# A hybrid decoder layer on one core: start-up transfers, two projection tiles ahead of the norm, and the within-chunk products of RWKV and HGRN spread over four array quarters

## The chip, the cores and the metric

One core of one Trainium2 chip runs the whole program. The metric is device time in microseconds (us); the median of the runs counts. The engines are named as the profile names them: PE is TensorE's matmul stream, PEld its weight loads, DVE VectorE, ACT ScalarE, POOL GpSimd, SP the queue that issues the DMAs. Each engine runs its own instructions in a fixed order.

## The reference

One decoder layer over a prompt of 2048 tokens and 8 single-token samples, width 1024, all in float32:

```python
h = rmsnorm(x, norm_mix)
p = h @ w_in                                   # 1024 -> 31 tiles of 128 columns, and 12 columns more (b and a of GDN)
y_a = gdn_mixer(p_a); y_b = rwkv_mixer(p_b); y_c = hgrn_mixer(p_c)
x = x + concat(y_a, y_b, y_c) @ w_out
h = rmsnorm(x, norm_ffn)
x = x + (silu(h @ w_gate) * (h @ w_up)) @ w_down
y = rmsnorm(x, norm_final)
```

The three mixers are recurrences with heads of 64, done in chunks of 64 tokens (6, 6 and 4 heads). GDN and RWKV need per chunk the inverse of a unit triangular 64x64 matrix, and all three need products of one chunk's tokens with the same chunk's tokens under a causal mask (in the reference of HGRN: `att = einsum('bhid,bhjd,bhijd->bhij', q, k, dec)`, then `att @ v`). GDN starts with a causal convolution over four tokens, and RWKV mixes each token with the one before, so both look back over the border of a group of tokens; ahead of the first token there are zeros.

## The kernel before

**Tiling.** Tokens stand on the free axis, in four groups q of 512 (the last has the 8 samples as well: 520, as two column ranges of 260). The input projection has 31 tiles m of 128 output columns for each q. A gemm tile (gemm8, L377 to L379) is 8 slices k of the contraction by 3 matmuls, since each float32 operand is split into a high and a low part (hi by hi, hi by lo, lo by hi; 128x512 each); ACT makes the high part of a weight (L332) or of x (L409), DVE the low one (L333, L410). Its result p is multiplied by the norm's 1/rms on DVE (L473) and stored to DRAM (s_p, L480), from where the units load slices. The statistics of the norm (stats_x) are eight squares added up (L456, L460), split (L495, L496) and summed over partitions by matmuls with ones (pni, L499 and L500), then Ln and Exp on ACT (L297, L300). In the same function stand the twelve extra columns (psb, L438, four column strips of the array; then the chain `ba`).

**Units.** For each q there are 3 GDN units (names in _g), 3 RWKV units (_r) and 2 HGRN units (_h); a unit has two heads, one on partitions 0 to 63, one on 64 to 127. Its chunk products are 64x64 or 64x128 matmuls in plain float32, each of which stands as two records in the trace. The matmul of head h reads rows of its half, and its result lies in the half of the output partitions that the head after it needs: a quarter of the array (row half, column half). RWKV: `att` (L1035) is run twice in a row, once for a3 (bank pa, same halves, so the two quarters of one diagonal), then, after the inverse is started, for k3 (bank pk, halves swapped: the other diagonal); each runs twice over four chunks and is masked by DVE (L1052, L1054). HGRN: 5 levels, each with 8 chunks of two 64x64 products (pl, L260 by `pair`), all on one diagonal, into one bank that DVE copies under a mask (L1217).

**Order.** A Driver interleaves the units with the gemm stream. In a turn each live unit goes one step (to its next yield), and then the gemm stream makes products until it has RATES[q] more (12.25 to 19.25 matmuls per turn). A scheduler fixes the order on each engine from that. When all units have ended, the rest of the gemm stream (late) runs by itself, with weights in the units' T buffers; until then gemms come from three banks (tag g) and S buffers.

**Start.** dram() sets 3 columns of zeros before each projected tile of q = 0 by one DMA (L205, 12 bytes at a time, `s_p<-zero`). Then SP issues what the program's text and the scheduler order: the first weight, x, constants, the sample buffers (cbuf, pbuf, o_cs), weights of w_out, x of q = 1, and only then tile 1's weights.

## Time and profile before

| | us |
|---|---|
| median of 3 runs (3198.95 to 3200.74) | 3200.33 |
| profiled execution, its own time | 3198.47 |
| span of that execution | 3196.7 |
| PE busy | 3085.4 (97%) |
| DVE busy | 2192.8 (69%) |
| ACT busy | 1189.0 (37%) |
| mean granted clock of TensorE | 0.983 |

The time lies 1.8 us above the span; the median lies 1.9 us above the profiled execution. A matmul's duration in the rows holds its way through the array, so successive ones overlap: what one costs is the distance of their starts. In rows of a timeline, x16 is the number of records that stand together, and the time in brackets is the idle time before them and who ended it.

### The profile page before, as it was taken

The page shows a single profiled execution, that of the slowest core. Times are in us where ns is not written, and L with a number is a line of the kernel's source. Part 1 is how long each engine was busy: PE and PEld are TensorE (multiplying, and loading weights), DVE is VectorE, ACT ScalarE, POOL GpSimd, SP SyncE. Part 2 cuts the span into 40 slices and gives each one's busy share as a digit, 9 for nine tenths or more (in the row PEclk, how much of TensorE's full clock was granted, in tenths as well). Part 3 has the DMA queues.
Part 4 walks back from the last instruction along what each step waited for, and adds up shares of the span by engine and source line. Part 5 has one row for each costly group of instructions (what it writes and reads, how often), then busy time and mean ns, then how long its engine had stood idle before and what let it go on. Part 6 is the DMA issues. An engine that isn't in the chain of part 4 may idle for free.

```text
span 3196.7 us, 62530 instructions
## 1 busy us (share of the span) xinstructions
PE 3085.4 (97%) x24812; PEld 2469.9 (77%) x24812; DVE 2192.8 (69%) x5369; ACT 1189.0 (37%) x2056; POOL 10.2 (0%) x21
## 2 busy tenths in 40 slices
PE   5989999999999999999999999999999999999998
PEld 3767767777888767677777777777777778999998
DVE  4885666678667788986898887778766654443334
ACT  3543143235325444644365435254532312221002
POOL 0000000000000000000000000000000000000000
PEclk8989999999999999999999999999999999999999
DMA  9958657656655766677775445565645456755552
GB/s 233 333 187 272 186 177 215 187 167 183 198 162 184 229 212 204 221 226 251 227 226 185 162 158 170 168 184 183 205 162 165 149 207 210 249 173 185 185 185 90
DMA packets 393074, 628.06 MB, mean 196 GB/s; under 512 B 176653, under 2 KB 181005, under 8 KB 392781
## 3 DMA queue, kind: packets, MB, share of 16 engines
q1 hardware_dynamic: 391692, 622.99, 61.0%
q8 instruction: 195, 3.19, 0.4%
q10 hardware_dynamic: 1088, 1.07, 0.1%
q14 instruction: 99, 0.80, 0.1%
HBM read 456.79 MB, written 167.19 MB: 195 GB/s over the span
## 4 chain that ended last, share of the span: by engine, by line
PE 79%; DVE 9%; DMA 6%; ACT 3%; SPq 1%; issue 1%; DVEq 0%; ACTq 0%
PE psp L377 7%; PE psp L378 7%; PE psp L379 7%; PE pd L377 5%; PE pd L378 5%; PE pd L379 5%; PE pfu L378 5%; PE pfg L377 4%; PE pfu L377 4%; PE pfu L379 4%; PE pfg L378 4%; PE pfg L379 4%; PE pso L378 1%; PE pso L377 1%; PE pso L379 1%
## 5 line engine op out<-in xcount | busy, mean ns | idle before, releaser
L377 PE MATMUL psp<-xs,w_in 128*128 128x512 f32 (+1 forms) x1240 | 446.3, 360 | 29.2 <-ACT xs L409 17.5
L378 PE MATMUL psp<-xs,w_in 128*128 128x512 f32 (+1 forms) x1240 | 445.9, 360 | 0.3 <-DVE xs L410 0.3
L379 PE MATMUL psp<-xs,w_in 128*128 128x512 f32 (+1 forms) x1240 | 442.9, 357 | 0.8 <-DVE w_in L333 0.8
L377 PEld LDWEIGHTS psp<-xs,w_in 128*128 128x128 f32 x1240 | 235.5, 190 | 72.6 <-ACT xs L409 19.7
L379 PEld LDWEIGHTS psp<-xs,w_in 128*128 128x128 f32 x1240 | 235.6, 190 | 39.5 <-issue 4.4
L378 PEld LDWEIGHTS psp<-xs,w_in 128*128 128x128 f32 x1240 | 235.4, 190 | 39.1 <-issue 2.9
L591 DVE TENSOR_TENSOR x<-pd,x 128x512 f32<-128x512 f32 (+1 forms) x240 | 138.3, 583 | 115.6 <-PE pd L379 113.9
L377 PE MATMUL pfg<-xhs,w_wg 128*128 128x512 f32 x496 | 201.8, 407 | 3.9 <-ACT w_wg L332 2.3
L379 PE MATMUL pfu<-xhs,w_wu 128*128 128x512 f32 x496 | 198.7, 401 | 1.4 <-DVE w_wu L333 1.2
L378 PE MATMUL pfg<-xhs,w_wg 128*128 128x512 f32 x496 | 198.6, 400 | 0.7 <-DVE xhs L549 0.7
L378 PE MATMUL pfu<-xhs,w_wu 128*128 128x512 f32 x496 | 199.2, 402 | 0.0
L377 PE MATMUL pfu<-xhs,w_wu 128*128 128x512 f32 x496 | 198.6, 400 | 0.3 <-ACT w_wu L332 0.3
L379 PE MATMUL pfg<-xhs,w_wg 128*128 128x512 f32 x496 | 198.0, 399 | 0.8 <-DVE w_wg L333 0.8
L377 PE MATMUL pd<-u,w_wd 128*128 128x512 f32 x464 | 188.3, 414 | 6.4 <-ACT u L362 2.3
L378 PE MATMUL pd<-u,w_wd 128*128 128x512 f32 x464 | 187.2, 404 | 0.4 <-DVE u L363 0.2
L379 PE MATMUL pd<-u,w_wd 128*128 128x512 f32 x464 | 185.1, 400 | 0.0
L570 ACT ACTIVATE t<-t 128x512 f32<-128x512 f32 (+1 forms) x110 | 60.0, 546 | 305.3 <-DVE t L569 301.7
L286 ACT ACT_TABLE_LOAD x91 | 116.8, 1283 | 113.6 <-PE oss_g L276 22.1
L362 ACT ACTIVATE u<-t 128x512 fp32r<-128x512 f32 (+1 forms) x110 | 59.9, 545 | 221.1 <-DVE t L573 220.2
L473 DVE TENSOR_TENSOR p<-psp,ri 128x512 f32<-128x512 f32 (+1 forms) x155 | 90.3, 583 | 73.2 <-PE psp L379 71.3
L572 DVE SCALAR_TENSOR_TENSOR t<-pfu,rf 128x512 f32<-128x512 f32 (+1 forms) x110 | 64.2, 583 | 102.9 <-PE pfu L379 100.0
L569 DVE TENSOR_TENSOR t<-pfg,rf 128x512 f32<-128x512 f32 (+1 forms) x110 | 64.2, 584 | 91.3 <-PE pfg L379 83.2
(638 smaller groups left out, 7368.9 us busy)
## 6 DMA issues: line engine op xcount, KB each, us to landing
w_in<-sw_in SPq DMA_DIRECT2D x186, 512.0 KB, 3.9
w_wg<-sw_wg SPq DMA_DIRECT2D x80, 512.0 KB, 3.5
w_wu<-sw_wu SPq DMA_DIRECT2D x80, 512.0 KB, 3.3
w_wd<-sw_wd SPq DMA_DIRECT2D x72, 512.0 KB, 3.3
sw_in<-w_in SPq DMA_DIRECT2D x62, 512.0 KB, 5.1
s_p<-p SPq DMA_DIRECT2D x93, 256.0 KB, 4.3
sw_wg<-w_wg SPq DMA_DIRECT2D x44, 512.0 KB, 2.9
sw_wu<-w_wu SPq DMA_DIRECT2D x44, 512.0 KB, 3.7
```

The source lines that it names most:

```text
L286: p = self.nc.scalar.preload_act_table_set("natural_log_exp_and_others")
L362: nc.scalar.activation(out[:, 0], src, AF.Copy)
L377: nc.tensor.matmul(ps, lhsT=hi[:, ws], rhs=xs[:, 0, xc], start=start, stop=False)
L378: nc.tensor.matmul(ps, lhsT=hi[:, ws], rhs=xs[:, 1, xc], start=False, stop=False)
L379: nc.tensor.matmul(ps, lhsT=lo[:, ws], rhs=xs[:, 0, xc], start=False, stop=stop)
L473: nc.vector.tensor_tensor(p[:, c0:c0 + cn], ps, rstd[q][:, c0:c0 + cn], ALU.mult)
L569: nc.vector.tensor_tensor(g, psg, r[:, cs], ALU.mult)
L570: nc.scalar.activation(t, g, AF.Tanh, scale=0.5)
L572: nc.vector.scalar_tensor_tensor(p, psu, 0.5, r[:, cs], ALU.mult, ALU.mult)
L591: nc.vector.tensor_tensor(x2[d][:, c0:c0 + cn], ps, x2[d][:, c0:c0 + cn], ALU.add)
```

## The change

1. **No zeros through DRAM.** The DMA in dram() goes; slice_p sets the 1 or 3 columns ahead of the group by a memset on POOL where q is 0, and loads only the 512 columns.
2. **Order of the first transfers.** The load of x of the next group moves to just ahead of the second unit's tiles (i == 1); it, the sample buffers and each first load of weights other than w_in's are issued only behind `mark`, the last s_p store made so far.
3. **Two tiles ahead.** For q = 0 the matmuls of the first two projection tiles stand ahead of stats_x in the program's text; their results are held in two banks until 1/rms is there. The buffers of pba, be and ba for q = 0 come from T instead of S.
4. **Four quarters.** RWKV's two products over four chunks are issued together, a diagonal into bank pa and the other into pk, by turns; HGRN's even chunks go on one diagonal into pl0, the odd ones on the other into pl1. Each RWKV unit has two yields fewer. HGRN's masked copy is split into two (even and odd chunks), and so are the copies into W.

```diff
-        zero = self.T("zero")[:, 0:HALO * N_IN]
-        self.nc.vector.memset(zero, 0.0)
-        self.nc.sync.dma_start(self.s_p[0][:, :, 0:HALO].rearrange("m p j -> p m j"),
-                               zero.rearrange("p (m j) -> p m j", j=HALO))
...
-                nc.sync.dma_start(raw, src[:, 512 * i:512 * i + 512])
+                with ExitStack() if key[0] == "in" else self.tc.issue_after(self.mark.ins):
+                    nc.sync.dma_start(raw, src[:, 512 * i:512 * i + 512])
...
-        p = self.S(f"pba{q}")
+        new = self.S if q else self.T
+        p = new(f"pba{q}")
...
-                ps = self.gemm8(w, xs[q], c0, cn, f"psp{q}_{m}_{c0}")
+                ps = held[0] if held else self.gemm8(w, xs[q], c0, cn, f"psp{q}_{m}_{c0}")
...
-            nc.sync.dma_start(self.s_p[q][m, :, HALO:], p[:, :n])
+            self.mark = nc.sync.dma_start(self.s_p[q][m, :, HALO:], p[:, :n])
...
-        self.nc.sync.dma_start(p[:, 0:halo + G], self.s_p[q][m, :, HALO - halo:HALO + G])
+        none = halo if q == 0 else 0
+        if none:
+            self.nc.gpsimd.memset(p[:, 0:none], 0.0)
+        self.nc.sync.dma_start(p[:, none:halo + G], self.s_p[q][m, :, HALO - halo + none:HALO + G])
...
+            for c0 in range(0, GC, 4):
+                cs = slice(c0, c0 + 4)
+                pa, pk = (self.ps(f"p{x}_{nm}").rearrange("p (c w i) -> p c w i", w=2, i=C) for x in "ak")
+                for c in range(4):
+                    for ps, l3, swap in ((pa, a3, 0), (pk, k3, 1)):
                         for h in range(2):
-                            p, o = slice(64 * h, 64 * h + 64), 64 * (h ^ swap)
-                            nc.tensor.matmul(ps[o:o + 64, c], lhsT=l3[p, c0 + c], rhs=rk[p, :, c0 + c],
+                            nc.tensor.matmul(ps[H[h ^ swap], c], lhsT=l3[H[h], c0 + c], rhs=rk[H[h], :, c0 + c],
                                              start=True, stop=True)
...
-                ps = ch(self.ps(f"pl_{nm}"))
+                ps = [self.ps(f"pl{i}_{nm}")[:, :G // 2].rearrange("p (c i) -> p c i", i=C) for i in range(2)]
                 for c in range(GC):
-                    self.pair(lambda p: ps[p, c], lambda p: x3[p, c], lambda p: x3[p, c])
-                nc.vector.copy_predicated(att, self.bc(self.msk[:, n]), ps)
+                    for h in range(2):
+                        nc.tensor.matmul(ps[c % 2][H[h ^ c % 2], c // 2], lhsT=x3[H[h], c], rhs=x3[H[h], c],
+                                         start=True, stop=True)
+                for i in range(2):
+                    nc.vector.copy_predicated(att[:, i::2], self.bc(self.msk[:, n], GC // 2), ps[i])
...
-            if q < 3:
-                load[q + 1] = K.load_x(q + 1)
+            held = []
             for i, (ms, _) in enumerate(order):
+                if i == 1 and q < 3:
+                    with K.tc.issue_after(K.mark.ins):
+                        load[q + 1] = K.load_x(q + 1)
...
+                        held = [K.gemm8(w, xs[q], 0, G, f"psp{q}_{m}")]
+                        w2 = K.load_w(K.io["w1"][ms[1]], ("in", ms[1]), 0)
+                        second = K.gemm8(w2, xs[q], 0, G, f"psp{q}_{ms[1]}")
                         K.load_consts()
+                        K.proj((q,), m, xs, rstd, None, lambda: K.stats_x(0, load[0]), held)
+                        held, w = [second], None
```

**SP at the start.** Before, the rows from tile 0's x to tile 1's first weight (rw_in_0_384; raw_x_262 to 271 are x of q = 1; sw_in is the split weight that is stored for later groups):

```order
L331 DMA rw_o_0_12234<-wo 128x512
L331 DMA rw_o_0_12241<-wo 128x512
L188 DMA blk<-blk 128x256
L194 DMA msk<-msk 128x320
L397 DMA raw_x_262<-xT 128x512 x2
L397 DMA raw_x_265<-xT 128x512 x2
L397 DMA raw_x_268<-xT 128x512 x2
L397 DMA raw_x_271<-xT 128x512 x2
L476 DMA s_p_148<-p_0_274 128x3
L480 DMA s_p_147<-p_0_274 128x512
L756 DMA s_be_142<-be_351 6x512
L331 DMA rw_in_0_384<-w 128x512
```

Here tile 1's weights stand behind the stores of p and be (L476 to L756). After, from the second half of x on:

```order
L337 DMA sw_in_0_1_221<-w_in_0_216 128x1024
L394 DMA raw_x_232<-xT 128x512 x2
L328 DMA rw_in_0_285<-w 128x512
L328 DMA rw_in_0_292<-w 128x512
L186 DMA cst<-cst 128x352
L188 DMA blk<-blk 128x256
L190 DMA w2a_113<-w 64x384
L191 DMA w2a_113<-a 64x384
L192 DMA g_114<-g 128x384
L194 DMA msk<-msk 128x320
L420 DMA wba<-wba 128x8x12
L328 DMA rw_in_0_412<-w 128x512
```

Tile 1's weights (rw_in_0_285, 292) follow x directly, the constants and wba follow them, and the loads of x for q = 1, of the sample buffers and of w_out have left this stretch.

**PE at the start.** Before, from the end of tile 0 (psp_0) to the start of tile 1:

```order
L377 MATMUL psp_0_0_275<-xs_7_259,w_in_0_219 128x512
L438 MATMUL psb_0_337<-raw_x_226,wba 12x512 x2
L438 MATMUL psb_0_337<-raw_x_229,wba 12x512 x2
L438 MATMUL psb_0_337<-raw_x_232,wba 12x512 x2
L438 MATMUL psb_0_337<-raw_x_235,wba 12x512 x2
L378 MATMUL psp_0_0_275<-xs_7_259,w_in_0_219 128x512
L379 MATMUL psp_0_0_275<-xs_7_259,w_in_0_219 128x512
L499 MATMUL pni_330<-sqhi_326,ones 128x512
L500 MATMUL pni_330<-sqli_327,ones 128x512
L377 MATMUL psp_1_0_398<-xs_0_238,w_in_0_383 128x512
```

After, the same place:

```order
L375 MATMUL psp_0_259<-xs_7_256,w_in_0_216 128x512
L376 MATMUL psp_0_259<-xs_7_256,w_in_0_216 128x512
L374 MATMUL psp_1_298<-xs_0_235,w_in_0_284 128x512
L375 MATMUL psp_1_298<-xs_0_235,w_in_0_284 128x512
L436 MATMUL psb_0_371<-raw_x_223,wba 12x512 x2
L436 MATMUL psb_0_371<-raw_x_226,wba 12x512 x2
L436 MATMUL psb_0_371<-raw_x_229,wba 12x512 x2
L436 MATMUL psb_0_371<-raw_x_232,wba 12x512 x2
L376 MATMUL psp_1_298<-xs_0_235,w_in_0_284 128x512
L374 MATMUL psp_1_298<-xs_1_238,w_in_0_284 128x512
```

The statistics' matmuls (pni) stood ahead of tile 1; now 22 matmuls of tile 1 stand ahead of them, and psb stands in tile 1.

**PE in an RWKV unit.** After, two groups of four chunks of one unit (pa_r_2805 is the first, pa_r_2886 the second; before, pa and pk of a group stood apart everywhere); first the end of the interleaved one and the start of the other:

```order
L1052 MATMUL pk_r_2806<-kr_r_2606,kr_2603 64x128 x2
L1052 MATMUL pa_r_2805<-kr_r_2606,a_r_2554 64x128 x2
L1052 MATMUL pk_r_2806<-kr_r_2606,kr_2603 64x128 x2
L1052 MATMUL pa_r_2805<-kr_r_2606,a_r_2554 64x128 x2
L1052 MATMUL pk_r_2806<-kr_r_2606,kr_2603 64x128 x2
L374 MATMUL psp_5_0_4450<-xs_2_3299,w_in_1_4445 128x512
L256 MATMUL pS_r_2872<-SA_r_1980,bt_r_1473 64x64 x2
L375 MATMUL psp_5_0_4450<-xs_2_3299,w_in_1_4445 128x512
L714 MATMUL pj_g_2742<-N_g_1993,uT_g_2515 32x32 x16
L1052 MATMUL pa_r_2886<-kr_r_2606,a_r_2554 64x128 x8
L376 MATMUL psp_5_0_4450<-xs_2_3299,w_in_1_4445 128x512
```

Its second diagonal comes some twenty rows further on:

```order
L1128 MATMUL po_r_3406<-W_r_1303,Z_r_1278 64x64
L1105 MATMUL px_r_2910<-Z_r_1278,W_r_1301 64x64
L1052 MATMUL pk_r_2887<-kr_r_2606,kr_2603 64x128 x8
L1105 MATMUL px_r_2910<-Z_r_1279,W_r_1302 64x64
L1128 MATMUL po_r_3406<-W_r_1304,Z_r_1279 64x64
```

So one group goes by turns over four quarters, and the other as two runs of one diagonal each.

**PE at the end of the units.** Before, the last HGRN level of the last unit (pl_h) and an RWKV chunk step (px_r):

```order
L379 MATMUL pd_7_28274<-u_12_27880,w_wd_3_2_28258 128x512
L377 MATMUL pd_7_28274<-u_13_27984,w_wd_3_2_28258 128x512
L378 MATMUL pd_7_28274<-u_13_27984,w_wd_3_2_28258 128x512
L379 MATMUL pd_7_28274<-u_13_27984,w_wd_3_2_28258 128x512
L260 MATMUL pl_h_28295<-lv_h_28250 64x64 x3
L1101 MATMUL px_r_28288<-Z_r_26158,W_r_26383 64x64
L1101 MATMUL px_r_28288<-Z_r_26159,W_r_26384 64x64
L260 MATMUL pl_h_28295<-lv_h_28250 64x64 x13
L377 MATMUL pfg_14_28322<-xhs_0_25377,w_wg_2_28313 128x512
```

After, the last steps of the same units up to the first gemm behind them (pfg_12, the gate product of the first tile that takes its weights hw_wg from T buffers):

```order
L1223 MATMUL pl_h_27890<-lv_h_27859 64x64 x8
L1223 MATMUL pl_h_27891<-lv_h_27859 64x64 x8
L1128 MATMUL po_r_28054<-W_r_25776,Z_r_25720 64x64
L1105 MATMUL px_r_27817<-Z_r_25720,W_r_25774 64x64
L1105 MATMUL px_r_27817<-Z_r_25721,W_r_25775 64x64
L1128 MATMUL po_r_28054<-W_r_25777,Z_r_25721 64x64
L725 MATMUL ptk_h_27999<-cst,kx_h_27958 128x128 x4
L256 MATMUL pv_r_27830<-X_r_27820,N_r_25772 64x64 x2
L256 MATMUL pS_r_27854<-SA_r_26827,bt_r_26151 64x64 x2
L1128 MATMUL po_r_28054<-W_r_25776,Z_r_25720 64x64
L1105 MATMUL px_r_27883<-Z_r_25720,W_r_25774 64x64
L1105 MATMUL px_r_27883<-Z_r_25721,W_r_25775 64x64
L1128 MATMUL po_r_28054<-W_r_25777,Z_r_25721 64x64
L374 MATMUL pfg_12_28427<-xhs_0_26006,hw_wg_2_28378 128x512
```

Before, gemms (pd_7, pfg_14) stand on both sides of the units' rows; after, 75 rows of units with no gemm among them end here, and the units end at tile 11 of the feed-forward of q = 2 instead of tile 17.

## Rows read from the trace of the kernel before

**Rows 1.** The page: busy time of the engines, and three lines of the 40 slices of the span (tenths of each slice; PEclk is the granted clock).

```profile
PE 3085.4 (97%) x24812; PEld 2469.9 (77%) x24812; DVE 2192.8 (69%) x5369; ACT 1189.0 (37%) x2056; POOL 10.2 (0%) x21
...
PE   5989999999999999999999999999999999999998
...
DVE  4885666678667788986898887778766654443334
...
PEclk8989999999999999999999999999999999999999
```

**Rows 2.** The page: the chain that ended last, shares by engine.

```profile
PE 79%; DVE 9%; DMA 6%; ACT 3%; SPq 1%; issue 1%; DVEq 0%; ACTq 0%
```

**Rows 3.** Timeline of SP's issues, 0 to 50 us (start, duration, line, operation, output from input, count). Here and in the other timelines rows of one kind in a row are one line.

```profile
3.25 0.38 SPq L205 DMA_DIRECT2D s_p<-zero  x1
3.68 8.69 SPq L397 DMA_DIRECT2D raw_x<-xT  x2
...
32.32 4.30 SPq L397 DMA_DIRECT2D raw_x<-xT  x8
44.27 0.33 SPq L476 DMA_DIRECT2D s_p<-p  x1
...
45.59 2.30 SPq L331 DMA_DIRECT2D rw_in<-w  x4
```

**Rows 4.** Timeline of PE, 2 to 62 us.

```profile
7.27 0.79 PE L377 MATMUL psp<-xs,w_in 128*128 128x512 f32 x1 [7.27 <-ACT xs L409]
...
21.51 0.80 PE L377 MATMUL psp<-xs,w_in 128*128 128x512 f32 x1 [7.90 <-ACT xs L409]
...
28.40 1.91 PE L438 MATMUL psb<-raw_x,wba 128*12 128x512 f32 x16
...
38.02 0.80 PE L499 MATMUL pni<-sqhi,ones 128*128 128x512 f32 x1 [7.05 <-DVE sqhi L495]
...
49.98 0.79 PE L377 MATMUL psp<-xs,w_in 128*128 128x512 f32 x1 [9.85 <-ACT w_in L332]
...
59.23 0.40 PE L378 MATMUL psp<-xs,w_in 128*128 128x512 f32 x1
```

**Rows 5.** Timeline of DVE, 5 to 62 us.

```profile
28.98 3.88 DVE L460 TENSOR_TENSOR acci<-acci,sqi 128x512 f32<-128x512 f32 x5 [0.29 <-ACT sqi L456]
...
37.56 0.41 DVE L495 CAST sqhi<-acci 128x512 fp32r<-128x512 f32 x1
...
43.55 0.69 DVE L473 TENSOR_TENSOR p<-psp,ri 128x512 f32<-128x512 f32 x1
```

**Rows 6.** Windows of 10 us from 0 to 80 us: length, busy time of each engine with count, granted clock, DMA share, GB/s; the sum is that of all eight.

```profile
30.00:40.00 10.00, 2.42 (x8) 0.87 (x4) 7.94 (x14) 2.69 (x5) 0.00 (x0) 0.80 0.93 272
40.00:50.00 10.00, 0.15 (x2) 0.02 (x1) 3.88 (x7) 7.66 (x10) 0.00 (x0) 0.50 0.46 143
...
sum 80.00, PE 43.96 PEld 29.56 DVE 38.39 ACT 28.42 POOL 1.01; mean PE 5.50 PEld 3.69 DVE 4.80 ACT 3.55 POOL 0.13
```

**Rows 7.** Windows of the stretch 166 to 197 us, the same columns.

```profile
166.00:176.00 10.00, 9.02 (x235) 6.07 (x235) 9.65 (x21) 4.86 (x9) 0.00 (x0) 1.00 0.14 37
176.00:186.00 10.00, 4.89 (x80) 3.38 (x73) 9.76 (x28) 4.17 (x8) 0.00 (x0) 0.67 0.16 18
186.00:197.00 11.00, 7.22 (x60) 5.02 (x59) 10.72 (x30) 7.89 (x13) 0.00 (x0) 0.50 0.52 157
```

**Rows 8.** Timeline of PE in that stretch: its first row, a run of one diagonal, and the first gemm behind it.

```profile
165.96 0.60 PE L724 MATMUL ptv_r<-cst,vr 128*128 128x128 f32 x4
...
172.58 1.09 PE L1045 MATMUL pk_r<-kr_r,kr 64*64 64x128 f32 x16
...
196.96 0.79 PE L377 MATMUL psp<-xs,w_in 128*128 128x512 f32 x1
```

**Rows 9.** Timeline of PE, 594 to 597 us: an HGRN level, and a GDN product on the other diagonal (it is the product pv, whose halves are swapped).

```profile
595.00 0.27 PE L260 MATMUL pl_h<-lv_h 64*64 64x64 f32 x1
595.00 0.27 PE L888 MATMUL pv_g<-X_g,N_g 64*64 64x64 f32 x2
...
595.12 1.60 PE L260 MATMUL pl_h<-lv_h 64*64 64x64 f32 x47
```

**Rows 10.** Timeline of PE, 700 to 712 us: two gemm matmuls, a small product, and the next gemm matmul.

```profile
708.81 0.40 PE L378 MATMUL psp<-xs,w_in 128*128 128x512 f32 x1
709.04 0.39 PE L379 MATMUL psp<-xs,w_in 128*128 128x512 f32 x1
709.37 0.33 PE L260 MATMUL pv_r<-X_r,N_r 64*64 64x64 f32 x4
709.63 0.50 PE L377 MATMUL psp<-xs,w_in 128*128 128x512 f32 x1
```

**Rows 11.** The instructions of the tile pa_r (engine, operation, count, duration in ns least/median/most, first and last start, shapes); pk_r has as many.

```profile
L1045 PE MATMUL pa_r<-kr_r,a_r x384: 269/269/320, 169.4 to 2394.1; 64*64 64x128 f32 x192
```

**Rows 12.** The instructions of the tile pl_h, and of the copy from it.

```profile
L260 PE MATMUL pl_h<-lv_h x1280: 218/218/364, 595.0 to 2604.5; 64*64 64x64 f32 x183
L1217 DVE COPY_PREDICATED att_h<-msk,pl_h x40: 685/727/759, 596.3 to 2604.8; 128x512 f32<-128x512 uint8 x40
```

**Rows 13.** Windows of 80 us in the mix of units and gemms, and near its end.

```profile
1280.00:1360.00 80.00, 74.95 (x628) 55.49 (x626) 72.12 (x167) 48.91 (x81) 0.00 (x0) 1.00 0.71 226
...
2560.00:2640.00 80.00, 80.00 (x587) 62.19 (x586) 44.82 (x105) 11.28 (x19) 0.31 (x1) 1.00 0.59 206
```

More of the change, by code (lines that the diff above doesn't have):

```diff
@@ L752, in ba @@
         h = slice(0, 12)
-        a, b = p[h, :n], self.S(f"be{q}")[h, :n]
+        new = self.S if q else self.T
+        a, b = p[h, :n], new(f"be{q}")[h, :n]
         nc.scalar.activation(b, a, AF.Tanh, scale=0.5)
@@ L757, in ba @@
         nc.vector.tensor_scalar(a, a, self.par("dtb")[h], None, ALU.add)
-        w1, w2, w3 = (self.S(f"ba{q}_{i}")[h, :n] for i in range(3))
+        w1, w2, w3 = (new(f"ba{q}_{i}")[h, :n] for i in range(3))
         made = nc.vector.scalar_tensor_tensor(w1, a, -1.0, a, ALU.mult, ALU.min)
@@ L1036, in first @@
             fb = f[:, :, None].to_broadcast([128, GC, C])
-            def att(l3, swap, outs, name):
-                for c0 in range(0, GC, 4):
-                    ps = self.ps(f"p{name}_{nm}").rearrange("p (c w i) -> p c w i", w=2, i=C)
-                    for c in range(4):
+            N, Rb = (ch(self.T(f"{n}_{nm}")) for n in ("N", "Rb"))
+            W = [[ch(self.T(f"W{w}{h}_{nm}")) for h in range(2)] for w in range(2)]
+            for c0 in range(0, GC, 4):
[3 more added lines that the diff above has]
+                    for ps, l3, swap in ((pa, a3, 0), (pk, k3, 1)):
@@ L1055, in att, with out @@
-                    yield
-            NR = [ch(self.T(f"{n}_{nm}")) for n in ("N", "Rb")]
-            yield from att(a3, 0, lambda w: ((NR[w], slice(0, 128)),), "a")
-            N, Rb = NR
+                def out(to, ps, w, p):
+                    m = lambda x: x[p, None, :].to_broadcast([p.stop - p.start, 4, C])
+                    if w == 0:
+                        nc.vector.tensor_tensor(to[:, cs], ps[p, :, w], m(self.nstrict), ALU.mult)
+                    else:
+                        nc.vector.scalar_tensor_tensor(to[:, cs], m(self.neg), 0.0, ps[p, :, w], ALU.is_ge, ALU.mult)
@@ L1060, in first @@
+                for w, to in enumerate((N, Rb)):
+                    out(to, pa, w, slice(0, 128))
+                for w in range(2):
+                    for h in range(2):
+                        out(half(W[w], h, True), pk, w, H[1 - h])
+                yield
             inv = self.inverse(N, ("r", u, q), nm)
@@ L1062, in first @@
             yield
-            W = [[ch(self.T(f"W{w}{h}_{nm}")) for h in range(2)] for w in range(2)]
-            yield from att(k3, 1, lambda w: [(half(W[w], h, True), slice(64 - 64 * h, 128 - 64 * h))
-                                             for h in range(2)], "k")
             nc.vector.tensor_tensor(k3, k3, fb, ALU.mult)
@@ L1224, in first @@
                 nc.vector.tensor_tensor(half(W, h), ch(q)[H[h]], ch(eb)[H[h]], ALU.mult)
-                nc.vector.tensor_copy(half(W, h, True), att[H[h]])
+                for i in range(2):
+                    nc.vector.tensor_copy(half(W, h, True)[:, i::2], att[H[h ^ i], i::2])
             ends = self.sp.tile([128, GC], F32, tag="he", name=f"he_{nm}")
@@ L1514, in gemm @@
                 for m in ms:
-                    K.proj((q,), m, xs, rstd, w, lambda: K.stats_x(0, load[0]))
                     if w:
+                        held = [K.gemm8(w, xs[q], 0, G, f"psp{q}_{m}")]
+                        w2 = K.load_w(K.io["w1"][ms[1]], ("in", ms[1]), 0)
+                        second = K.gemm8(w2, xs[q], 0, G, f"psp{q}_{ms[1]}")
                         K.load_consts()
-                    w = None
+                        K.proj((q,), m, xs, rstd, None, lambda: K.stats_x(0, load[0]), held)
+                        held, w = [second], None
+                    else:
+                        K.proj((q,), m, xs, rstd, None, None, held)
+                        held = []
                     have[0] += 1
```

20 lines of the change are left out of this document (7 added, 13 removed).

## The prediction

> **What bounds the kernel now.** I read the page first: PE is busy 3085.4 of 3196.7 us, so 111 us are idle and the rest goes only if PE's own work gets shorter [rows 1]. The chain that ended last says the same, 79% of it on PE and 9% on DVE [rows 2]. The slices show where the idle time is: PE starts at 5 tenths, and DVE is at 8 or 9 tenths in the middle [rows 1]. The windows of the first 80 us have PE busy for 43.96, so 36 of the 111 us are lost there [rows 6]. A second hole is at 166 to 197 us, 31 us without a gemm, in which PE's windows add up to 21.1 of 31 us while DVE is busy 30.1 of 31 [rows 7, 8]. The other 65 us or so are spread over the mix, where DVE comes near its limit: PE 74.95 of 80 us with DVE at 72.12, but 80 of 80 with DVE at 44.82 [rows 13]. So three prices matter: the start, PE's work in small products, and stretches in which DVE paces.
>
> **The start.** The timeline of SP shows x held up: the two issues behind the zeros' DMA take 8.69 us [rows 3]. PE waits for x until 21.51, then for the squares until 38.02, and then for tile 1's weights until 49.98 [rows 4]; these are issued at 45.59, behind x of q = 1 (4.30 us) and the store of p at 44.27 [rows 3]. Without the zeros, 3 MB (two weight tiles and x) at the 272 GB/s of the window from 30 us [rows 6] need 11 us from 2 us on: x is in at about 12 and split at 14. The squares then need what they need now, from the last of x's matmuls near 27 to 37.56, about 10.4 us [rows 4, 5], and some 2.5 us more, since ACT and DVE split tile 1's weights in between: 27. From the first of the statistics' matmuls to p of tile 0 it is now 38.02 to 43.55, 5.5 us [rows 4, 5], so p comes at about 32.5. By then tile 1's 24 matmuls (11 us even at twice the warm spacing of 0.23 [rows 10]) are done beside the squares, and tile 2 can use tile 0's bank at 33. Before, tile 2 is where PE stands at 59.2 [rows 4]. That is 26 us; 4 off for a cold clock (0.80 and 0.50 in the windows in which PE waits [rows 6]) and for the split of the next weights: **-22**, from -12 (if psb, whose weights now come behind the constants, and the squares hold tile 1 up) to -30 (if the statistics don't stretch). The memsets on POOL, idle all but 10.2 us [rows 1], cost nothing. Nor do the transfers that move behind the last store: x of q = 1 is first read by the statistics that end in the hole at 166 us, the sample buffers later still; on SP they now stand behind more weights. The T buffers of the ba chain take it off the S buffers into which SP loads raw weights.
>
> **The hole at 166 us.** After's order has 48 steps of units without a gemm there instead of 33, but 195 matmuls for 188. At 30.1 us of DVE for 79 instructions [rows 7], 0.38 each, some dozen more on the chain are **+5** (0 to +10).
>
> **Four quarters.** A full-array product of 128 columns costs about 0.11 us a record (4 in 0.60, less the last one's way of 0.27), and a 64x128 record on a diagonal 55 ns (16 in 1.09, less 0.27, over 15) [rows 8]: two quarters run at once already. An HGRN record costs 30 ns (47 in 1.60, less 0.22, over 46) [rows 9]. That four run at once the trace shows at one place only: at 595.00 records of pl_h and of pv_g, on the other diagonal, start in the same hundredth [rows 9]. If they do, a record's price halves: RWKV has 2 x 384 records [rows 11], 768 x 27 ns = 21 us, HGRN 1280 x 15 ns = 19 us [rows 12]. But only what stands by turns in the order gains. Counted through PE's order, about 7 of 24 RWKV groups' worth does (the others are two runs of eight, as in the example), 6.3 us, and 27 of 40 HGRN levels, 12.6 us: **-19**, from 0 (not at once) to -25.
>
> The Trainium skill, "TensorEngine Tiling (Array Packing)", Restrictions and Gotchas, says that different row tiles cannot access the same PSUM bank at the same time. The pairs of pk_r write one bank from two row halves and go at half the full array's price [rows 8], so it doesn't hold in this trace for a diagonal. By the rule each of the two banks would take one quarter at a time, the sum would lose the 19, and the time would be that of rival E.
>
> **Fewer interruptions.** A pair between two gemm matmuls takes 0.59 us from start to start instead of 0.23, 0.36 more; its four records at 30 ns are 0.12 of that, so each change of shape costs about 0.12 [rows 10]. PE's order has 1457 such changes after for 1552 before: 95 x 0.12 = **-11** (-5, if DVE paces at those places, to -20, if the pairs' own latency goes too).
>
> **DVE in a shorter mix.** The masked copies become 80 of half the width for 40 of 727 ns [rows 12], and 16 copies become 32: between nothing and 29 us more DVE work, and I take 8, for a half costs more than half. With 24 turns fewer some 380 gemm matmuls (24 x 16, near 89 us) leave the mix for the late stretch, so the same DVE work stands in less time. PE idles 5 us in 80 where DVE is at 72, and none at 45 [rows 13]; four per cent more load on the some 900 us between give **+8** (0 to +20). That both banks of a lane are now filled in one step, so the next step's products wait for the masks, is in this term.
>
> **The uncovered end of the units.** Before, gemms stand on both sides of the last levels, and PE is busy 80 of 80 us at 2560 to 2640 [rows 13]. After, the 75 rows up to pfg_12 have no gemm: pfg_12's weights need T buffers that the units free last, and their loads stand on SP behind the stores of y_g and of the HGRN state. Their DVE chain is some 60 to 90 instructions. At the 0.38 us of the hole [rows 7] that is 23 to 34 us; PE's own work in it is 9 us: **+15**, from +8 (part of it hidden by records of the units themselves) to +25.
>
> **Sum.** -22 + 5 - 19 - 11 + 8 + 15 = -24 against the profiled 3198.5, or 3174.5; the median lies 1.9 above it, so **3176**.
>
> **Rivals.** A is the forecast, with its terms some 15 us either way: 3160 to 3192.
>
> B, the uncovered stretches cost little: DVE +0, hole +0, end +8, the rest as in the sum: -44, 3156; with the start and the interruptions at their best (-30, -20) 3139. For it speaks that DVE is at 69% in the mean [rows 1]; against it that the hole of 166 us is DVE-paced now [rows 7].
>
> C, DVE decides: what PE saves in products is not on the path where DVE is at 72 of 80 [rows 13], and DVE +20, hole +10, end +25 stand against the 52 of gains: 3203. For it speaks that the added copies are on DVE. The Trainium skill, same page, Performance Considerations, says that tiling speeds TensorE and not the emptying of PSUM, which may become the bottleneck; the rows show this only where DVE is above some 65 of 80.
>
> D, slower by the gemm-less end alone: fewer turns let the units outlive their gemms. With the other terms as forecast (-39) it must cost over 45 us to pass 3206.7, that is, a stretch of 54 us with 9 us of PE in it. At the hole's pace, 31 us for 33 steps [rows 7, 8], its 45 steps are 42 us, 33 lost: 3194. It needs a third more than that pace, as when the weights' loads wait and the clock falls to the 0.50 of 186 to 197 us [rows 7]: 3210.
>
> E, the change doesn't do what it says: four quarters don't run at once; the quarters' term is 0: 3195.
>
> **How the numbers follow.** A 0.58, B 0.14, C 0.12, D 0.08, E 0.08. A difference under 0.2% (6.4 us) can hardly be told from none here. Faster (below 3193.9) are A, B, and a third of E and C: 0.79. Within are most of the rest of E and half of C: 0.11. Slower are D and a little of C: 0.10. The range 3146 to 3198 leaves out D, most of C and B's best end, together about 0.2.
>
> **What would show it.** Start: PE busy in the first 80 us rises from 44 to about 64, tile 2's matmuls begin near 33, and no wait for w_in precedes tile 1. Quarters: a run of pa and pk by turns takes some 27 ns a record, 16 ns for pl; if 55 and 30, E. End: a gap in the gemms around 2500 us, about 24 us long, with DVE full; if over 50, D. DVE: windows at 1280 to 1360 with PE below 73 would speak for C. The forecast is wrong if the start's wait moves to the squares or psb as a whole, or if the new order opens holes in the mix that the old one had not.

## The result and the profile after

The changed kernel takes 3220.23 us in the median of four runs (3218.68 to 3222.8), the kernel before 3199.64 on the same chip; the ratio is 1.007, with a 95% interval of 1.0053 to 1.0088. Measured a second time it was 1.0063 (1.0048 to 1.0078). So the change is slower by 21 us where 24 us faster was forecast. Measured again beside each group of experiments, the kernel before had medians of 3190 to 3194 us; each ratio is to the one beside it. Executions of one kernel differ by up to some 20 us, the shorter ones with the higher mean granted clock (e13 below: 3166 and 3168 us at 0.986, the other five 3176 to 3182 us at 0.981 or 0.982), and each split below is that of one profiled execution.

The page after, with the lines that answer to [rows 1, 2]:

```profile
PE 3079.2 (96%) x24812; PEld 2464.1 (77%) x24812; DVE 2194.7 (68%) x5424; ACT 1176.6 (37%) x2051; POOL 12.1 (0%) x41
...
PE   8999999989998999999999999999999899999998
...
PEclk9989999999998999999999999999999899999999
...
PE 68%; DVE 14%; DMA 9%; ACT 4%; issue 2%; SPq 2%; DVEq 0%; ACTq 0%
```

PE is busy 6 us less, and its share of the chain is 11 points less, while DVE's, DMA's and issue's shares have grown. A busy PE is not PE at full speed, so I split each trace into windows of 5 us and counted as lost in each: the idle time of PE, and its busy time times (1 - granted clock), called cold below. What is left is work at full clock. By stage, in us:

| profiled execution | span | 0-80 | 80-240 | 240-2480 (mix) | 2480-2880 (end of the units) | from 2880 | work at full clock |
|---|---|---|---|---|---|---|---|
| before | 3196.7 | 39.5 | 18.2 | 69.8 | 6.7 | 12.7 | 3049.7 |
| after | 3218.8 | 14.6 | 23.0 | 107.2 | 43.6 | 12.2 | 3018.2 |
| difference | +22.1 | -24.9 | +4.8 | +37.4 | +36.9 | -0.5 | -31.5 |

Three of the forecast's terms are there: the start (-22 forecast, -24.9), the hole at 166 us (+5, +4.8) and PE's work (-19 and -11 forecast, -31.5). Two stages eat it all, the mix and the end. Of the mix's +37.4, 13.0 us lie at 1000 to 1070 us (18.4 lost after, 5.4 before), in the hole that is read below; the other 24 are spread, 10 of them at 640 to 800 us (19.2 against 9.4). In idle time and cold clock, the mix lost 49.1 + 20.7 before and 75.5 + 31.8 after.

**The start.** Windows, and PE's and DVE's timelines of the changed kernel, against [rows 4 to 6]:

```profile
10.00:20.00 10.00, 7.60 (x22) 5.02 (x21) 5.76 (x10) 6.71 (x13) 0.00 (x0) 1.00 1.01 318
20.00:30.00 10.00, 8.94 (x39) 4.96 (x40) 9.86 (x18) 3.31 (x6) 0.00 (x0) 0.83 0.96 350
30.00:40.00 10.00, 10.00 (x45) 8.10 (x44) 5.88 (x11) 7.00 (x10) 0.00 (x0) 1.00 0.87 333
```

```profile
8.36 0.79 PE L374 MATMUL psp<-xs,w_in 128*128 128x512 f32 x1 [8.36 <-ACT xs L406]
...
21.06 0.80 PE L374 MATMUL psp<-xs,w_in 128*128 128x512 f32 x1 [3.16 <-ACT w_in L329]
...
22.22 2.96 PE L436 MATMUL psb<-raw_x,wba 128*12 128x512 f32 x16
...
30.33 0.39 PE L500 MATMUL pni<-sqhi,ones 128*128 128x512 f32 x1
...
30.79 0.39 PE L374 MATMUL psp<-xs,w_in 128*128 128x512 f32 x1
```

```profile
25.59 0.42 DVE L496 CAST sqhi<-acci 128x512 fp32r<-128x512 f32 x1
...
34.57 1.29 DVE L471 TENSOR_TENSOR p<-psp,ri 128x512 f32<-128x512 f32 x2
```

Tile 1 starts at 21.06 instead of 49.98, tile 2 at 30.79 directly behind the statistics' matmuls (it doesn't wait for p of tile 0, as the forecast had it), and that p comes at 34.57 instead of 43.55 (32.5 was forecast). All 24 matmuls of tile 1 stand ahead of the statistics'. Tile 1 still waits 3.16 us for its weights, where the forecast had no such wait as a sign of being right. PE is busy 66.8 us of the first 80, for 44 before.

**The quarters.** An HGRN level of the changed kernel on PE, and its masked copy:

```profile
578.37 0.69 PE L1223 MATMUL pl_h<-lv_h 64*64 64x64 f32 x32
```

```profile
L1226 DVE COPY_PREDICATED att_h<-msk,pl_h x80: 412/442/455, 580.0 to 2566.2; 128x256 f32<-128x256 uint8 x80
```

32 records in 0.69 us, less the last one's 0.22, are 15 ns each where 30 were [rows 9]: four quarters run at once. A run of pa and pk by turns:

```profile
149.71 0.33 PE L1052 MATMUL pa_r<-kr_r,a_r 64*64 64x128 f32 x2
149.76 0.33 PE L1052 MATMUL pk_r<-kr_r,kr 64*64 64x128 f32 x2
...
150.55 0.30 PE L1052 MATMUL pk_r<-kr_r,kr 64*64 64x128 f32 x2
```

These are 32 records in 1.14 us, less 0.27 for the last one's way: 27 to 28 ns a record, for 55 [rows 8]. The copy of half the width takes 442 ns, so a pair costs 157 more than the 727 of [rows 12], 6.3 us in all; with 32 copies of 289 ns for 16 of 422 it is 8.8, and the forecast took 8. DVE's busy time as a whole rose by 1.9 us only (2192.8 to 2194.7).

**The first loss: ahead of w_out.** SP and PE around 1015 us, in the changed kernel:

```profile
1015.75 0.32 SPq L478 DMA_DIRECT2D s_p<-p  x1
1016.12 0.43 SPq L1416 DMA_DIRECT2D cbuf<-cbuf  x1
1016.60 4.68 SPq L1417 DMA_DIRECT2D pbuf<-pbuf  x1
...
1023.21 1.83 SPq L515 DMA_DIRECT2D mxs<-s_mix  x4
1025.09 0.97 SPq L328 DMA_DIRECT2D rw_o<-wo  x2
```

```profile
1013.76 0.28 PE L376 MATMUL psp<-xs,w_in 128*128 128x260 f32 x1
...
1027.04 0.80 PE L272 MATMUL oss_g<-lo_oss_g,blkr 128*128 128x512 f32 x1 [0.84 <-DVE lo_oss_g L270]
1033.51 0.79 PE L374 MATMUL pso<-mxs,w_o 128*128 128x512 f32 x1 [5.67 <-ACT w_o L329]
```

The last projection matmul starts at 1013.76, and the next gemm at 1033.51. SP first stores the last p (1015.75), and only then the transfers that the change holds behind it: the sample buffers, of which pbuf takes SP 4.68 us, then loads of the mixed heads (mxs, w_out's other operand), and w_out's first weights at 1025.09. These must land and be split, and pso (w_out's product) waits 5.67 us for that. The granted clock is 0.50 from 1020 to 1040 us. In the kernel before SP issues these transfers in the first 32 us:

```profile
25.21 0.38 SPq L1405 DMA_DIRECT2D cbuf<-cbuf  x1
25.92 3.45 SPq L1406 DMA_DIRECT2D pbuf<-pbuf  x1
...
30.14 1.05 SPq L331 DMA_DIRECT2D rw_o<-wo  x2
```

There the last projection matmul starts at 1056.13 and pso at 1058.94.

**The second loss: the units without gemms.** Windows, SP and PE at 2535 to 2575 us:

```profile
2540.00:2550.00 10.00, 3.08 (x61) 2.14 (x61) 9.78 (x30) 4.66 (x8) 0.00 (x0) 0.67 0.09 26
2550.00:2560.00 10.00, 4.54 (x80) 4.10 (x80) 9.46 (x30) 1.13 (x2) 0.00 (x0) 0.50 0.09 31
2560.00:2570.00 10.00, 8.28 (x105) 6.71 (x100) 8.75 (x27) 1.71 (x4) 0.00 (x0) 0.50 0.46 155
```

```profile
2558.54 0.34 SPq L1429 DMA_DIRECT2D o_hp<-st_h  x1
2562.50 0.32 SPq L342 DMA_DIRECT2D hw_wg<-sw_wg  x1
```

```profile
2534.42 0.50 PE L376 MATMUL pfu<-xhs,w_wu 128*128 128x512 f32 x1
...
2545.54 0.48 PE L256 MATMUL pv_r<-X_r,N_r 64*64 64x64 f32 x4 [3.29 <-DVE X_r L1107]
...
2554.27 1.61 PE L1223 MATMUL pl_h<-lv_h 64*64 64x64 f32 x32 [3.61 <-DVE att_h L1226]
...
2569.57 0.80 PE L374 MATMUL pfg<-xhs,hw_wg 128*128 128x512 f32 x1
```

From the gemm at 2534.4 to the one at 2569.57 PE has only the units' rows, and DVE is busy 9.78 and 9.46 of 10 us; PE waits for it (att_h, X_r). The weights hw_wg are issued at 2562.50, behind the stores. The gap is 34.7 us long, PE is busy in it for 19.2 us at a mean clock of 0.62, and DVE runs 97 instructions in 32.6 us. The windows of 2535 to 2580 us lost 25.0 us: 15.5 idle and 9.5 of cold clock, some 2 of them in the gemms behind the gap.

A second, shorter gap follows, and the windows of 2600 to 2640 us lost 11.7 more, 7.4 idle and 4.3 cold:

```profile
2604.08 0.40 PE L376 MATMUL pd<-u,lw_wd 128*128 128x512 f32 x1
...
2608.98 1.97 PE L1270 MATMUL po_h<-W_h,Z_h 128*64 128x64 f32 x32 [2.71 <-ACT osq_h L293]
...
2616.37 0.80 PE L374 MATMUL pd<-u,hw_wd 128*128 128x512 f32 x1 [1.74 <-DVE t L570]
```

Here the last unit makes its output (osq_h, y_h), and the next gemm waits for DVE to empty the bank of pfg (t, L570), which stands behind that output in DVE's order. Neither gap is in the kernel before, which loses nothing from 2480 to 2640 us.

### The profile page after: what moved, and what is told of

Same layout as the page of the kernel before. It is cut to its first block, busy times and chain, and to the rows that moved or that the text cites. A ratio compares the mean times of both kernels' runs of the same rounds, so it can differ in the third digit from the quotient of the medians.

```text
span 3218.8 us, 62719 instructions
## 1 busy us (share of the span) xinstructions
PE 3079.2 (96%) x24812; PEld 2464.1 (77%) x24812; DVE 2194.7 (68%) x5424; ACT 1176.6 (37%) x2051; POOL 12.1 (0%) x41
## 4 chain that ended last, share of the span: by engine, by line
PE 68%; DVE 14%; DMA 9%; ACT 4%; issue 2%; SPq 2%; DVEq 0%; ACTq 0%
PE psp L374 5%; PE psp L376 5%; PE psp L375 5%; PE pd L374 4%; PE pd L375 4%; PE pd L376 4%; PE pfg L374 4%; PE pfg L376 4%; PE pfu L375 4%; PE pfu L374 4%; PE pfu L376 4%; PE pfg L375 4%; DMA rw_wu<-wu 1%; PE pso L374 1%; PE pso L375 1%
## 5 line engine op out<-in xcount | busy, mean ns | idle before, releaser
L374 PEld LDWEIGHTS psp<-xs,w_in 128*128 128x128 f32 x1240 | 236.1, 190 | 60.2 <-ACT xs L406 9.0
L374 PE MATMUL pfg<-xhs,w_wg 128*128 128x512 f32 x448 | 181.0, 404 | 4.3 <-ACT w_wg L329 3.4
L375 PE MATMUL pfg<-xhs,w_wg 128*128 128x512 f32 x448 | 180.6, 403 | 2.5 <-DVE xhs L550 2.5
L374 PE MATMUL pd<-u,w_wd 128*128 128x512 f32 x432 | 173.5, 409 | 9.1 <-ACT w_wd L329 3.2
L376 PE MATMUL pfg<-xhs,w_wg 128*128 128x512 f32 x448 | 180.5, 403 | 0.3 <-DVE w_wg L330 0.3
L374 PE MATMUL pfu<-xhs,w_wu 128*128 128x512 f32 x448 | 180.1, 402 | 0.0
L375 PE MATMUL pfu<-xhs,w_wu 128*128 128x512 f32 x448 | 180.0, 402 | 0.0
L376 PE MATMUL pfu<-xhs,w_wu 128*128 128x512 f32 x448 | 179.6, 401 | 0.0
L375 PE MATMUL pd<-u,w_wd 128*128 128x512 f32 x432 | 173.7, 403 | 1.6 <-DVE u L360 1.6
L376 PE MATMUL pd<-u,w_wd 128*128 128x512 f32 x432 | 172.2, 400 | 1.5 <-DVE w_wd L330 1.4
L375 PE MATMUL pd<-u,hw_wd 128*128 128x260 f32 (+1 forms) x448 | 137.6, 308 | 0.0
L376 PE MATMUL pd<-u,lw_wd 128*128 128x260 f32 (+1 forms) x448 | 137.1, 308 | 0.0
```

Of the source, the lines that this page charges most:

```text
L374: nc.tensor.matmul(ps, lhsT=hi[:, ws], rhs=xs[:, 0, xc], start=start, stop=False)
L375: nc.tensor.matmul(ps, lhsT=hi[:, ws], rhs=xs[:, 1, xc], start=False, stop=False)
L376: nc.tensor.matmul(ps, lhsT=lo[:, ws], rhs=xs[:, 0, xc], start=False, stop=stop)
```

## The experiments

All ratios are to the kernel before as measured beside the run, with their 95% intervals. The split is that of above. Its one execution lies off the median of the kernel's executions here and there: 11 us above the median in e10, 7 above in e4, 7 below in e3.

| kernel | ratio | span | 0-80 | 80-240 | mix | end | work at full clock |
|---|---|---|---|---|---|---|---|
| e0 the change again | 1.0063 (1.0048 to 1.0078) | 3209.4 | 14.3 | 21.1 | 101.9 | 42.4 | 3017.9 |
| e1 transfers behind the first store | 0.9987 (0.9972 to 1.0001) | 3191.9 | 17.2 | 23.0 | 82.2 | 30.5 | 3023.7 |
| e2 two steps back | 0.9944 (0.9928 to 0.9961) | 3172.3 | 14.1 | 21.7 | 99.7 | 5.2 | 3018.9 |
| e3 both | 0.9898 (0.9883 to 0.9912) | 3152.8 | 18.0 | 23.7 | 64.0 | 6.4 | 3027.3 |
| e4 start alone | 1.0043 (1.0027 to 1.0058) | 3209.8 | 16.0 | 25.8 | 94.6 | 5.4 | 3055.3 |
| e5 quarters alone | 1.0041 (1.0027 to 1.0056) | 3207.3 | 37.7 | 16.1 | 81.4 | 46.3 | 3013.6 |
| e6 start alone, first store | 0.9945 (0.9930 to 0.9960) | 3174.8 | 18.8 | 24.0 | 62.3 | 4.9 | 3052.4 |
| e7 as e2, diagonals apart | 0.9990 (0.9978 to 1.0001) | 3182.9 | 16.2 | 20.2 | 85.2 | 6.7 | 3042.6 |
| e8 as e4, samples early | 0.9996 (0.9984 to 1.0008) | 3186.4 | 19.4 | 17.0 | 75.0 | 6.1 | 3056.4 |
| e9 as e4, weights early | 1.0009 (0.9995 to 1.0022) | 3188.8 | 18.0 | 13.7 | 85.8 | 5.8 | 3052.9 |
| e10 as e1, rates raised | 0.9971 (0.9951 to 0.9990) | 3191.4 | 18.0 | 26.1 | 94.4 | 19.4 | 3021.5 |
| e11 as e5, two steps back | 0.9985 (0.9974 to 0.9996) | 3187.1 | 36.7 | 16.1 | 84.3 | 6.0 | 3031.7 |
| e12 before, transfers held | 1.0045 (1.0031 to 1.0059) | 3203.3 | 36.3 | 20.3 | 84.4 | 6.3 | 3044.3 |
| e13 as e1, steps elsewhere | 0.9948 (0.9929 to 0.9967) | 3177.7 | 18.8 | 24.2 | 84.0 | 5.5 | 3032.2 |

**e0, the change again.** The changed kernel as it is.

> The change as it is, on the same chip as the others of this call: ratio to the kernel before 1.005 to 1.009 as first measured, with the hole ahead of the first pso and the gap near 2545 us.

1.0063, with both losses: 20.4 us lost at 1000 to 1070 us, and a gap of 34.6 us ahead of pfg. Its mix lost 101.9 where the first execution lost 107.2: so far apart are two executions of the same kernel. It is the base for the comparisons below.

**e1, transfers behind the first store.**

```diff
             self.mark = nc.sync.dma_start(self.s_p[q][m, :, HALO:], p[:, :n])
+            self.first = getattr(self, "first", self.mark)
...
-                with ExitStack() if key[0] == "in" else self.tc.issue_after(self.mark.ins):
+                with ExitStack() if key[0] == "in" else self.tc.issue_after(self.first.ins):
...
-        with self.tc.issue_after(self.mark.ins):
+        with self.tc.issue_after(self.first.ins):
```

> The changed kernel, but the sample buffers (cbuf, pbuf, o_cs) and the first loads of w_out's and the feed-forward's weights are issued behind the first store of p, and no longer behind the last one; x of the next group stays behind the last one. Theory H (held transfers: these loads reach SP only behind the last projection tile, just when w_out's first product wants them): the hole of about 20 us ahead of the first pso near 1015 us goes, with its cold clock some 20 us; the end of the units is untouched: about 3200. Theory T (fewer turns: all that is lost is lost where the units run out of gemms): the hole near 1015 us is a shift of the same order and comes back elsewhere, and the gap near 2545 us stays: 3215 to 3222. If both losses hang on the held transfers: about 3165.

24 us less than the change in ratio. The hole near 1015 us is gone (0.7 us lost in 1000 to 1070 us, 20.4 in e0), and the mix lost 82 instead of 102. SP issues w_out's first weights at 82.5 us. But the end was expected untouched and lost 30.5 for 42.4, as the gap there is 15.2 us instead of 34.6: the edit moved the order too. So theory H holds for the hole; that the time fell by about the expected 20 us is partly chance, for the end gave 12 more and the start and PE's work took 9 back.

**e2, two steps back.**

```diff
                         out(half(W[w], h, True), pk, w, H[1 - h])
                 yield
+                yield
```

> The changed kernel with two bare steps more in each RWKV unit, so that the Driver makes as many turns, and as many gemm matmuls beside the units, as before. Theory T (fewer turns): the gap of 35 us near 2545 us, 37 us with its clock, goes, and gemms cover the units to tile 17 of the feed-forward: about 3183. Theory H (held transfers): the hole near 1015 us stays, so no lower than 3183, and if the rest of the mix is as dense as it was, about 3200. Theory Q (the quarters themselves make DVE or the banks the bound): no change, 3215 to 3222.

The end's loss is gone, 43.6 to 5.2, and PE's order has 8472 gemms ahead of the last level as before. The window in this run:

```profile
1000.00:1070.00 70.00, 57.96 (x676) 46.76 (x676) 56.68 (x177) 32.54 (x60) 0.00 (x0) 0.85 0.60 173
2480.00:2640.00 160.00, 160.00 (x1066) 122.63 (x1065) 90.66 (x222) 34.74 (x53) 0.53 (x1) 1.00 0.53 176
```

PE is busy all of 2480 to 2640 us at full clock. The hole near 1015 us stands: the mix lost 99.7. The time fell by 38 us in ratio, as much as the end had lost. Theory T holds for this stage, and Q falls in the form recorded here (no change of the time); e11 comes back to it.

**e3, both.** The two edits above together.

> Both repairs: first transfers behind the first store of p, and two bare steps more in each RWKV unit. If the two losses are separate (held transfers, some 27 of the time between the change and the run with the first store; fewer turns, some 45 between the change and the run with the steps), the sum is not to be had whole, since either repair moves the rows of both: ratio to the kernel before 0.988 to 0.992, the hole ahead of the first pso and the gap near 2545 us both gone. If what the repairs gave was mostly another deal of the order, the ratio stays at that of the run with the steps, 0.994, or above.

0.9898, within what was expected. Of the mix 64 us are lost, no more than before the change (69.8). This version is 31 us faster than the kernel before, and the fastest of all.

**e4 and e6, the start alone.** The changed kernel with the functions for RWKV's and HGRN's products from the kernel before; e6 with e1's edit as well.

> The changed kernel with the within-chunk products, their masks and their steps as in the kernel before: only the start is changed (no zeros, order of the first transfers, two tiles ahead). The start alone should give 25 us (idle and cold PE time of the first 80 us: 39 before, 14 after). Theory H: the hole ahead of the first pso stays and takes about 20 back: about 3195. Theory T or Q: no hole, the gain stays: about 3175.

> The start alone, as in the run of the start alone (ratio 1.004), but with the first transfers behind the first store. Theory H: the hole of 15 us ahead of the first pso, 20 with its clock, goes: ratio 0.997 or a little above. If the start alone is slow for another reason (x of the next group and the stretch of 80 to 240 us, or the deal of the order): 1.002 to 1.005.

The start gives 24 and 21 us, and yet e4 is slower than before by 0.4%: neither expectation (3195 and 3175 us, ratios of 0.998 and 0.992) holds. The mix lost 94.6, of which 14.0 at 1000 to 1070 us. In e6, which came out better than expected, these windows are full:

```profile
1000.00:1070.00 70.00, 70.00 (x737) 57.19 (x736) 54.55 (x155) 30.74 (x59) 0.00 (x0) 1.00 0.74 233
```

The difference of the two ratios is 31 us: the largest price of the held transfers of the three pairs (e0 to e1 24, e2 to e3 15). In idle time and cold clock the mix goes from 62.7 + 31.9 in e4 to 49.3 + 13.0 in e6, so more than half of this pair's difference there is clock, and not the hole. In the other pairs it goes from 71.3 + 30.6 to 54.4 + 27.8 (e0 to e1) and from 73.0 + 26.8 to 48.9 + 15.1 (e2 to e3).

**e5 and e11, the quarters alone.** The kernel before with the functions of the change, e11 with e2's edit as well.

> The kernel before with the four quarters alone (products, masks, two steps fewer per RWKV unit); its start and its first transfers are those of before. PE's work at full clock should be some 31 us less, as in the changed kernel (3018 for 3050). Theory T: the end of the units, 8280 gemms instead of 8472 ahead of the last level and 89 rows without a gemm, takes 37 back or a little more: about 3205. Theory H: no hole near 1015 us and no gap that costs: about 3170. Theory Q (DVE and the banks): the mix is denser everywhere and gives back all: 3200 to 3215.

> The kernel before with the four quarters and the two bare steps more: start and transfers of before. Theory T: of the quarters alone (ratio 1.0041) the 39 us at the end of the units come back and the 31 of warm PE work show: 0.990 to 0.993. Theory Q (the quarters' masks and banks make the mix denser): above 0.997.

e5 came out as T said in its two parts: work at full clock 36 us less, the end 40 more lost; with the mix's 11.6 more the ratio is some 8 us above T's 3205 and within Q's range. In e11 the end is covered, 18 us of ratio come back, but not the 39: its work at full clock is 18 below before where e5's is 36, since its order has 1566 changes of shape on PE instead of 1448 (1552 before). And its mix lost 84.3 for 69.8. T's range (0.990 to 0.993) failed and Q's (above 0.997) held: the quarters do make the mix some 12 to 15 us dearer on this start (e5 +11.6, e11 +14.5). By the traces it is hardly the quarters' banks: PE's idle time right ahead of the records of pa, pk and pl, from 240 to 2480 us, adds up to 0.9 us before, 2.2 in the change, 1.5 in e3 and 1.0 in e11.

**e7, diagonals apart.**

```diff
-                for c in range(4):
-                    for ps, l3, swap in ((pa, a3, 0), (pk, k3, 1)):
+                for ps, l3, swap in ((pa, a3, 0), (pk, k3, 1)):
+                    for c in range(4):
                         for h in range(2):
...
-                for c in range(GC):
+                for c in (0, 2, 4, 6, 1, 3, 5, 7):
```

> The run with the two bare steps, but one diagonal behind the other: the eight products of pa and then the eight of pk, the even chunks of HGRN and then the odd ones; banks, masks and steps are as in that run. It prices the four quarters at once. Theory of the forecast (a by-turns product at half the price, 160 of 384 RWKV and 500 of 640 HGRN matmuls of that run, and 46 changes of shape at 0.12 to 0.2): 24 us plus 6 to 9 of warm PE work more, ratio some 0.0095 above that of the run with the steps, 1.004. If PE's small products lie beside DVE's work anyway: no difference.

Work at full clock is 23.7 us more than in e2, where 30 to 33 were priced (24 by halves, and 6 to 9 for 46 changes of shape). The time is only 0.46%, 15 us, more, about half of the 0.95% expected, and not the "no difference" of the other theory: the mix lost 85.2 for 99.7 in e2, so part of what going by turns saves on PE was spent waiting, or another order hides it.

**e8 and e9, samples or weights early.** e4 with the one half of e1's edit, and with the other.

> The start alone (ratio 1.0043 with all transfers behind the last store, 0.9945 with all behind the first), with only the sample buffers cbuf, pbuf and o_cs behind the first store, and the weights still behind the last. If the hole ahead of the first pso comes from the sample buffers on SP (pbuf holds SP for 4.7 us there, ahead of the mix's loads): ratio 0.995 to 0.997, the hole gone. If it comes from w_out's weights, which can't be split before they land: 1.001 to 1.004.

> The counterpart: the start alone with only the first loads of the weights behind the first store, and the sample buffers behind the last. If the sample buffers on SP make the hole: 1.001 to 1.004, the hole there. If the weights do: 0.995 to 0.997.

Neither expectation holds as it stands. In e8 the hole is there (14.5 us without a gemm ahead of the first pso, 15.1 in e4), in e9 it is not (4.6), so it is the held weights that make it:

```profile
1037.78 0.28 PE L376 MATMUL psp<-xs,w_in 128*128 128x260 f32 x1
...
1052.57 0.80 PE L374 MATMUL pso<-mxs,w_o 128*128 128x512 f32 x1 [2.05 <-ACT w_o L329]
```

```profile
1045.33 0.28 PE L376 MATMUL psp<-xs,w_in 128*128 128x260 f32 x1
...
1050.19 0.90 PE L374 MATMUL pso<-mxs,w_o 128*128 128x512 f32 x2 [2.96 <-ACT mxs L359]
```

The first two rows are e8's, the last two e9's. But of the 31 us in time the samples alone give 15 and the weights alone 11, which add up to 31 within the noise of some 6 us each, and e9 without the hole still lost 85.8 in the mix. What e8 gained there on e4 is mostly clock: 60.2 + 14.8, idle and cold, for 62.7 + 31.9. Why the held samples go with a colder mix stays open.

**e12, the held transfers alone**, in the kernel before (the `mark` and the two `issue_after` of the change, nothing else).

> The kernel before with one thing changed: the sample buffers and the first loads of the weights other than w_in's are issued behind the last store of p, as in the change. Theory H: a hole ahead of the first pso and a denser stretch around it, 22 to 36 us as between the held and the unheld versions; the start gets 1 to 4 us shorter as SP has less ahead of tile 1's weights: ratio 1.006 to 1.010. If the held transfers cost only together with the new start or were a matter of the deal: 0.998 to 1.003.

A hole of 21 us without a gemm ahead of the first pso, 14.1 lost at 1000 to 1070 us, the mix 14.6 more, the start 3.2 less. The ratio of 1.0045 is 14 us, between the two ranges expected. The mix's idle time and cold clock are 63.8 + 20.6, for 49.1 + 20.7 before: alone, the held transfers cost about the hole, in idle time. What the same edit gave beyond that in the pairs above is not the hole: in e1 the shorter gap at the end, in e6 the clock of the mix.

**e10 and e13, other ways to cover the end.** e1 with RATES = (12.95, 14.95, 15.95, 19.95), and e1 with two bare steps behind the start of the inverse.

> The run with the first store (ratio 0.9987, a gap of 15 us near 2535 us), with no steps added, but each of the Driver's four rates raised by 0.7 matmuls per turn, so that 8436 gemms instead of 8280 stand ahead of the last level (8472 before). Theory T (what counts is that gemms cover the units to their end): the end is covered as by the two bare steps, ratio 0.989 to 0.992. If the two steps helped by spreading the products of a unit over more turns: above 0.995.

> The run with the first store (0.9987) with the two bare steps put behind the start of the inverse, not between the groups of four chunks. 8472 gemms stand ahead of the last level, as in the run of both repairs (0.9898). Theory T as the number of turns at the old rates: 0.989 to 0.992. If the steps gave so much because they stand between the products: 0.995 or above, as with the raised rates (0.9971).

They lost 19.4 and 5.5 at the end for 30.5 in e1, and neither comes near e3: their mixes lost 94.4 and 84.0 for e3's 64.0. T's range (0.989 to 0.992) failed in both. So the number of gemms beside the units explains the end, as T said, and not the mix; e13 has the number of turns and 8472 gemms of e3 and is still 16 us behind it. The other expectation was that the steps help because they stand between the products: e10 is on its side (above 0.995), and e13, at 0.9948, at its edge. Waits for the products' banks are too small to be the reason: PE's idle time ahead of pa, pk and pl is 3.1 us in e13 and 1.5 in e3. In idle time and cold clock e13's mix lost 52.5 + 31.5 and e3's 48.9 + 15.1: the two differ by the granted clock, which also parts the executions of e13 from each other. What in the order decides on it stays open.

## Why the prediction was wrong

**The bound and the gains.** That PE's idle time lies in the start, a hole and the DVE-near mix was right in the main (of the 65 us that the prediction gave to the mix 16 lie behind 2480 us), and so were the start's term and mechanism (-22, measured -24.9, and in e4 and e6 -23.5 and -20.7), the hole at 166 us (+5, +4.8), and PE's work: -19 for the quarters and -11 for fewer changes of shape, together -30, measured -31.5 in work at full clock. e11 parts the two: with 14 more changes of shape than before its work is 18.0 us less, near the -19 of the quarters alone. By turns a record's price halves, so rival E is out. The rule of the Trainium skill that speaks for it ("TensorEngine Tiling (Array Packing)", Restrictions and Gotchas: no two row tiles in one PSUM bank at a time) disagrees with these runs: 15 and 27 ns a record are measured with two row halves writing each bank. e7 adds that of 24 us of such a gain, by turns and fewer changes together, 15 reached the time.

**The step that failed** first is the sentence that the transfers moved behind the last store cost nothing. It priced x and the sample buffers by when they are read, and left out w_out's weights, of which the diff says that they wait for the same store, and the mark itself: when w_out is first loaded, the last store so far is that of the last projection tile of the last group, directly ahead of w_out's first product. A prefetch that stood at 30 us on SP became a transfer on the chain at 1025 us. Measured: a hole of 14.5 to 21 us without a gemm ahead of the first pso in every version that holds the weights (the change, e2, e4, e7, e8, e12), none over 9 us in those that don't, and 14 us of time alone. The 15 to 31 us of the three pairs hold more than the hole.

**The end of the units** is the second step that failed: it had the right mechanism and the wrong size, +15 for 24 us without a gemm, less 9 of PE's work. Measured were 35 us without a gemm and 25.0 lost there, the upper bound of the term, and 11.7 more in the second gap, which the forecast didn't have; the stage as a whole lost 36.9 more. The DVE chain was counted at 60 to 90 instructions and priced at the low end of its 23 to 34 us; it has 97, at 0.36 us each. That PE's 9 us of work become 19 at the clock of the gap added little, for DVE sets the length: 35 less 9 is 26. Rival D was this mechanism, at 49 us and a chance of 0.08; it came at 37, and the held transfers made up the rest.

**DVE in a shorter mix**, +8: with the held transfers away the quarters cost the mix +2 (e6 to e3) to +20 (e6 to e1), and +12 to +15 on the old start. The bounds of 0 to 20 hold. It could not be told from what another order does, which moved the mix by 20 us between e3 and e13. Two of its parts were wrong: 192 gemm matmuls leave the mix (8280 for 8472 ahead of the last level), not 380; and the bound of some 65 of 80 that rival C reads for DVE isn't in the rows. In windows of 80 us of the kernel before, PE idles 3.0 us at 640 to 720 us with DVE at 59.75, and none at 1520 to 1600 us with DVE at 68.35.

The sum with the measured sizes: -24.9 + 4.8 - 31.5 + 37.4 + 36.9 - 0.5 = +22.2, and the spans differ by 22.1. It adds up by the way the split is made. Of the +37.4, 13.0 are the hole ahead of w_out; how the other 24 part among the quarters, the held transfers and the clock isn't shown.

## What to carry to other kernels

A transfer that is held behind "the last store so far" is held behind whatever that is when the consumer's code is emitted; look up in the order which instruction it is, and who wants the data next. Where a driver gives out work of one kind per step of another, leaving out steps leaves out cover: count what stands beside the last steps before and after, and price an uncovered stretch by counting the DVE instructions on its chain, less what PE does in it at full clock. Where two versions differ by 0.5%, split the loss into idle time and cold clock before giving it to an edit. A gain and a loss that come by different mechanisms are parted by undoing each alone, and here both undone beat either kernel.
